# Index scores of a sparse attention layer: pairs of heads, and the keys' low parts on 64 rows

## The chip, the cores and the metric

The kernel runs on one core of a Trainium2 chip. The metric is the device time of one execution in microseconds. The kernel before was timed in three runs: 1888.56, 1888.76 and 1889.16 us, median 1888.76. One further execution was profiled; every row of the trace comes from it.

## What is computed

Two layers of a decoder for 512 tokens of width 2048, in float32. The first layer is a sparse attention whose "indexer" scores every key for every query and keeps the best 128; the second is a stick-breaking attention. Only the indexer matters here:

```python
iq = partial_rope(iq.reshape(b, s, IDX_HEADS, IDX_DIM), positions, IDX_ROT)   # 16 heads of 64
ik = partial_rope(ik.reshape(b, s, 1, IDX_DIM), positions, IDX_ROT)[:, :, 0, :]
...
dots = jnp.einsum('bqhd,bsd->bqhs', iqb, ik).astype(jnp.float32)
iscore = jnp.einsum('bqhs,bqh->bqs', jax.nn.relu(dots), iwb.astype(jnp.float32)) * idx_scale
iscore = jnp.where(causal[None], iscore, -jnp.inf)
_, idx = lax.top_k(iscore, n_sel)
```

Sixteen index heads of dimension 64 share one set of 512 index keys. For each query the products with the keys go through a ReLU, are weighted per head, and summed over the heads. Since 128 keys are kept, the first 128 queries keep all that they may see, and scores are needed only for the queries from 128 on.

## The kernel before, in words

All activations are held transposed: the 128 partitions carry features, the free axis carries the tokens. Matmuls run on operands rounded to a shorter float32 format (fp32r). To keep float32 accuracy each operand is split into a high part, the rounded value, and a low part, the rest (`split`, L129): ScalarE makes the high part, VectorE subtracts. A product then takes three matmuls, high × high, high × low and low × high (`mm3`, L133, lines L134 to L136), which accumulate in one PSUM bank. There are eight banks of 128 × 512.

TensorE's instructions stand in the order in which the program writes them. The other engines' instructions are put in order by a planner, except those written as "paced". Two devices mix independent work into TensorE's stream: `interleave` (L57) runs a main generator and lets a second one, the fill, advance by a given total over the main one's steps; `pumped` (L313) hands out one queued piece of work on the other engines at each step. Weights come over the SP queue into three raw buffers, are split into `wh` and `wl` (three buffers each), and are prepared two pieces ahead.

The index stage goes as follows.

- The index queries come out of the projection as `iq`, two heads of 64 rows in a 128-row bank. `index_piece` (L573) turns them and makes, for each head, a stack `sa` or `sb` of 128 rows: for an even head rows 0 to 63 hold the high part and rows 64 to 127 the low part; for an odd head it is the other way round.
- The index keys `ik` (64 rows) are made into two operands of 128 rows, `B1` and `B2` (L648 to L651). `B1` holds the keys' high part in rows 0 to 63 and their low part in rows 64 to 127; `B2` holds them the other way round.
- `index_scores` (L665) runs over three blocks of 128 queries (i = 1, 2, 3), which see w = 256, 384 and 512 keys, and over the 16 heads. A head takes one of three banks in turn (`spare`, L531), two matmuls of the stack with `B1` and with `B2` (L671, L672), which together give all four products of the parts, then a ReLU by ScalarE into `rl` (three buffers) and an accumulation by VectorE into `am[i]`.
- The fill is the projection of the values, `gemm_x` (L292), on banks 4 to 7: 64 steps of three 512-wide matmuls each, tile `v` in the trace. 22 steps run ahead of the scores, 40 are spread over them, and the rest follows.
- Behind the stage come the splits of the values (`vh`, `vl`) and the projection of the queries (tile `q`), whose first group uses banks 0 to 3. Bank 3 was last used by the index queries.

In the trace the score banks are called `isc`, the operands `B1` and `B2` together `B`.

Of the kernel before, what the change touches and what calls it, by code (L numbers as in the profile page):

```python
# [10 lines left out]
F32 = mybir.dt.float32  # L11
F32R = mybir.dt.float32r
I32 = mybir.dt.int32
AF = mybir.ActivationFunctionType
ALU = mybir.AluOpType
# [3 lines left out]
T = 512  # L19
# [27 lines left out]
def run(gen):  # L47
    for _ in gen:
        pass


def steps(gen, n):
    for _ in range(n):
        next(gen, None)


def interleave(main, n_main, fill, n_fill, lead=0):  # L57

    steps(fill, lead)
    done = 0  # L60
    for i, _ in enumerate(main, 1):
        steps(fill, n_fill * i // n_main - done)
        done = n_fill * i // n_main
    run(fill)
# [13 lines left out]
def trunk_kernel(  # L78
# [17 lines left out]
    pe = nc.tensor  # L96
# [21 lines left out]
    act, dve, pool = (Paced(e) for e in (nc.scalar, nc.vector, nc.gpsimd))  # L118
# [7 lines left out]
    def bank(i, name="ps"):  # L126
        return psum.tile([128, 512], F32, name=name, tag=f"bank{i}")
# [5 lines left out]
    def mm3(out, a, b, start, stop):  # L133
        pe.matmul(out, a[0], b[0], start=start, stop=False)  # L134
        pe.matmul(out, a[0], b[1], start=False, stop=False)  # L135
        pe.matmul(out, a[1], b[0], start=False, stop=stop)  # L136
# [155 lines left out]
    def gemm_x(items, get, banks):  # L292

        for kb in range(NK):
            w = next(items)
            xh, xl = get(kb)
            for t, out in enumerate(banks):
                s = slice(t * 128, (t + 1) * 128)
                mm3(out, (xh[:, s], xl[:, s]), w, kb == 0, kb == NK - 1)
                yield  # L300
# [9 lines left out]
    def one():  # L310
        paced(bg.popleft())

    def pumped(gen, every=1):  # L313

        for i, _ in enumerate(gen):
            if bg and i % every == 0:
                one()
            yield

    def drain():  # L320
        while bg:
            one()
# [35 lines left out]
    def strassen_stream(widths, wp):  # L358
        return Ahead(strassen_items(widths, wp), 2)
# [73 lines left out]
    def first_chunk(gemm, TF, T1, C3, stream):  # L433

        for k in range(8):
            if k < 7:
                if k > 0:
                    paced(build_plain, k + 1)
            else:
                items = stream().prime()  # L440
            steps(gemm, 4)
            if k < 4:
                for piece in stream_sums(k + 4, TF[k % 2], T1[k + 4], C3):
                    paced(piece)
                    steps(gemm, 2)
            else:
                steps(gemm, 4)
            if k:
                paced(turn_first, k - 1, T1[k - 1])
        run(gemm)  # L450
        turn_first(7, T1[7])
        return items
# [78 lines left out]
    def spare(name, first=4):  # L531
        spin[0] = (spin[0] + 1) % 3
        return bank(first + spin[0], name)

    def mm_banks(name):
        return [bank(j, name) for j in range(4)]
# [4 lines left out]
    am = [pa.tile([128, 128 * (i + 1)], F32, name=f"am{i}") for i in range(4)]  # L541
# [5 lines left out]
    def all_items():  # L547
        yield from first_items()
        yield from plain_items([(80, NK), *[(512, NK)] * 10])

    items = Ahead(all_items(), 2)

    pi_ = ExitStack()
    ip = pi_.enter_context(ss(name="pi", bufs=1, side="right"))
    Ci = ip.tile([128, T], F32, name="Ci")
    Si = ip.tile([128, T], F32, name="Si")
    B1 = ip.tile([128, T], F32R, name="B1")
    B2 = ip.tile([128, T], F32R, name="B2")
    iws = ip.tile([128, 3, 16], F32, name="iws")
    stacks = {}  # L560
# [48 lines left out]
    def late_banks(where):  # L609
        return [bank(b, "iq")[:, :LATE] for b in where]  # L610
# [14 lines left out]
    banks = late_banks((4, 5, 6, 7))  # L625
# [11 lines left out]
    ps = bank(4, "ik")  # L637
    run(pumped(gemm_w(items, plain, [ps], 80)))
    drain()
    ik = ip.tile([128, T], F32, name="ik")  # L640
# [4 lines left out]
    dve.tensor_tensor(iksw[0:32], iksw[0:32], Si[0:32], ALU.mult)  # L645
    dve.tensor_tensor(ik[0:32], ik[0:32], Ci[0:32], ALU.mult)
    dve.tensor_tensor(ik[0:32], ik[0:32], iksw[0:32], ALU.add)
    act.activation(B1[0:64], ik[0:64], AF.Copy)  # L648
    act.activation(B2[64:128], ik[0:64], AF.Copy)
    dve.tensor_tensor(B1[64:128], ik[0:64], B1[0:64].bitcast(F32), ALU.subtract)  # L650
    dve.tensor_tensor(B2[0:64], ik[0:64], B1[0:64].bitcast(F32), ALU.subtract)  # L651

    banks = late_banks(range(4))
    gemm = gemm_w(items, late_plain, banks)
# [10 lines left out]
    def index_scores():  # L665
        for i in range(1, 4):
            w = 128 * (i + 1)
            for h in range(16):
                ps = spare("isc", 0)
                st = stacks[h][:, (i - 1) * 128 : i * 128]  # L670
                pe.matmul(ps[:, :w], st, B1[:, :w], start=True, stop=False)  # L671
                pe.matmul(ps[:, :w], st, B2[:, :w], start=False, stop=True)  # L672
                rl = ip.tile([128, T], F32, name="rl", tag="rl", bufs=3)
                act.activation(rl[:, :w], ps[:, :w], AF.Relu)
                wcol = iws[:, i - 1, h : h + 1]
                if h == 0:
                    dve.tensor_scalar(am[i], rl[:, :w], wcol, None, ALU.mult)
                else:
                    dve.scalar_tensor_tensor(am[i], rl[:, :w], wcol, am[i], ALU.mult, ALU.add)
                yield  # L680
            diag = am[i][:, i * 128 : w]
            pool.affine_select(out=diag, in_=diag, pattern=[[-1, 128]], compare_op=ALU.is_ge, fill=FILL, base=0, channel_multiplier=1)
        pool.memset(am[0], 0.0)
        pool.affine_select(out=am[0], in_=am[0], pattern=[[-1, 128]], compare_op=ALU.is_ge, fill=MASK, base=0, channel_multiplier=1)

    banks = [bank(b, "v") for b in (4, 5, 6, 7)]
    interleave(index_scores(), 48, pumped(gemm_x(items, plain, banks)), 40, lead=22)
    drain()
    pi_.close()
    pkv_ = ExitStack()  # L690
# [48 lines left out]
    for g in range(4):  # L739
        banks = [bank(b + 4 * (g % 2), "q") for b in range(4)]  # L740
# [61 lines left out]
    for g in range(4):  # L802
        banks = mm_banks("g")
# [267 lines left out]
    with ps_:  # L1071
# [3 lines left out]
        banks = [bank(b, "k") for b in range(4)]  # L1075
        gemm = gemm_w(kitems, plain, banks, order=PAIRS)
        items = first_chunk(gemm, TF, T1, C3, lambda: strassen_stream([512] * 5, sp))
# [45 lines left out]
    def gate_items():  # L1123
        for k, n in ((0, 6), (4, 2)):
            yield from plain_items([(512, n)])
            raw = next_raw()
            bg.extend(lambda raw=raw, k=k: restore(raw, k) for k in range(k, k + 4))
        yield from plain_items([(512, 8), *[(512, NK)] * 3])

    items = Ahead(gate_items(), 2)  # L1130
# [14 lines left out]
    banks = mm_banks("g")  # L1145
# [79 lines left out]
    for g in range(4):  # L1225
        tc.keep_in_program_order(act.preload_act_table_set("natural_log_exp_and_others"))
        if g:
            banks = mm_banks("g")
# [63 lines left out]
```

## Time and profile before

| | us |
|---|---|
| median of three runs | 1888.76 |
| the profiled execution's own time | 1889.62 |
| its span in the trace | 1887.9 |
| first score matmul | 144.57 |
| first matmul behind the last score matmul | 188.45 |

A row of a timeline gives the start and the duration in us, the engine, the line, the operation, out<-in by the program's names, the shapes and a count; in square brackets stands the idle time ahead of it and what ended it. PE is TensorE's matmuls and PEld its weight loads, which run beside them; DVE is VectorE, ACT ScalarE, POOL GpSimd. Instructions that a helper issues all carry the helper's line: L111 for everything on ScalarE and VectorE.

### The profile page before, as it was taken

To read this page: it belongs to the slowest core of one execution; us is meant where nothing else is said; L and a number is where in the kernel's file an instruction comes from. 1 tells how busy PE (TensorE), PEld (TensorE's weight loads), DVE (VectorE), ACT (ScalarE), POOL (GpSimd) and SP (SyncE) were. 2 spreads that over 40 slices of the span, in tenths; PEclk is the share of its full clock that TensorE was granted. 3 is DMA by queue.
4 is the path that set the end of the run, shared out by engine and by line. 5 is a ranking of instruction groups with operands and counts; after the bars stand their busy time and mean duration, and the time that the engine had idled before them with its cause. 6 is when DMAs were issued, how large, how long until landed. Compare 5 with 4: busy or idle time off the path is not lost.

```text
span 1887.9 us, 25064 instructions
## 1 busy us (share of the span) xinstructions
PE 1874.2 (99%) x9229; PEld 1584.7 (84%) x9229; DVE 1220.4 (65%) x2385; ACT 928.5 (49%) x1692; POOL 28.4 (2%) x49
## 2 busy tenths in 40 slices
PE   9999999999999999999999999999999999999998
PEld 7898888888888888888888999987888888888887
DVE  5668879966556454675368788876655545567534
ACT  4446323355554432474245444468877743347422
POOL 0000000000000000000000000000100000000000
PEclk9999999999999999999999999999999999999999
DMA  5432333312222532333343333331122153242333
GB/s 185 137 114 65 101 90 100 101 56 68 67 68 60 165 110 78 124 100 106 117 134 113 106 97 111 101 112 57 56 68 68 57 189 98 75 129 89 123 101 112
DMA packets 110587, 189.22 MB, mean 100 GB/s; under 512 B 8240, under 2 KB 28208, under 8 KB 110464
## 3 DMA queue, kind: packets, MB, share of 16 engines
q1 hardware_dynamic: 110320, 187.33, 32.3%
q8 instruction: 72, 1.18, 0.3%
q14 instruction: 51, 0.42, 0.1%
q0 software_dynamic: 144, 0.30, 0.1%
HBM read 179.21 MB, written 8.39 MB: 99 GB/s over the span
## 4 chain that ended last, share of the span: by engine, by line
PE 96%; DVE 2%; ACT 1%; DMA 1%; issue 1%; SPq 0%; DVEq 0%; ACTq 0%
PE g L134 12%; PE g L135 12%; PE g L136 12%; PE o L135 7%; PE o L136 7%; PE o L134 7%; PE m L134 3%; PE m L135 3%; PE m L136 3%; PE q L135 3%; PE q L136 3%; PE q L134 3%; PE z L1199 2%; PE k L136 2%; PE k L135 2%; PE k L134 2%
## 5 line engine op out<-in xcount | busy, mean ns | idle before, releaser
L111 ACT ACTIVATE wh<-raw 128x512 fp32r<-128x512 f32 (+3 forms) x684 | 396.4, 581 | 674.9 <-PE g L135 239.4
L111 DVE TENSOR_TENSOR wl<-raw,wh 128x512 fp32r<-128x512 f32 (+3 forms) x684 | 430.0, 630 | 430.9 <-ACT wh L111 411.6
L134 PE MATMUL g<-xh,wh 128*128 128x512 f32 x1024 | 404.3, 395 | 0.2
L135 PE MATMUL g<-xl,wh 128*128 128x512 f32 x1024 | 400.6, 391 | 0.6 <-DVE xl L111 0.6
L136 PE MATMUL g<-xh,wl 128*128 128x512 f32 x1024 | 399.9, 391 | 0.0
L134 PEld LDWEIGHTS g<-xh,wh 128*128 128x128 f32 x1024 | 192.6, 188 | 41.0 <-ACT sg L111 1.4
L136 PEld LDWEIGHTS g<-xh,wl 128*128 128x128 f32 x1024 | 192.2, 188 | 41.2
L135 PEld LDWEIGHTS g<-xl,wh 128*128 128x128 f32 x1024 | 192.5, 188 | 38.7 <-DVE xl L111 1.4
L136 PE MATMUL o<-xh,wl 128*128 128x512 f32 x512 | 199.3, 389 | 0.0
L135 PE MATMUL o<-xl,wh 128*128 128x512 f32 x512 | 199.2, 389 | 0.0
L134 PE MATMUL o<-xh,wh 128*128 128x512 f32 x512 | 199.2, 389 | 0.0
L136 PEld LDWEIGHTS o<-xh,wl 128*128 128x128 f32 x512 | 96.1, 188 | 20.3 <-DVE wl L111 0.4
L135 PEld LDWEIGHTS o<-xl,wh 128*128 128x128 f32 x512 | 96.1, 188 | 20.0
L134 PEld LDWEIGHTS o<-xh,wh 128*128 128x128 f32 x512 | 96.1, 188 | 19.9
L134 PE MATMUL q<-xh,wh 128*128 128x512 f32 x256 | 99.6, 389 | 0.0
L135 PE MATMUL q<-xl,wh 128*128 128x512 f32 x256 | 99.6, 389 | 0.0
L136 PE MATMUL q<-xh,wl 128*128 128x512 f32 x256 | 99.6, 389 | 0.0
L111 ACT ACTIVATE sh<-st 128x512 fp32r<-128x512 f32 x80 | 49.0, 628 | 79.7 <-PE m L135 42.5
L111 DVE TENSOR_TENSOR sl<-st,sh 128x512 fp32r<-128x512 f32 x80 | 54.5, 691 | 37.2 <-ACT sh L111 37.2
L111 DVE TENSOR_TENSOR xl<-f,xh 128x512 fp32r<-128x512 f32 x80 | 54.3, 687 | 11.4 <-ACT f L111 11.0
L111 ACT ACTIVATE wk<-z 128x512 f32<-128x512 f32 x80 | 47.3, 591 | 25.2 <-PE z L136 17.2
L134 PEld LDWEIGHTS q<-xh,wh 128*128 128x128 f32 x256 | 48.1, 188 | 10.1
(290 smaller groups left out, 3366.8 us busy)
## 6 DMA issues: line engine op xcount, KB each, us to landing
raw<-w_in_a SPq DMA_DIRECT2D x95, 512.0 KB, 3.7
raw<-w_in_b SPq DMA_DIRECT2D x64, 512.0 KB, 3.8
raw<-w_ple_gate SPq DMA_DIRECT2D x52, 512.0 KB, 3.8
raw<-w_o_a SPq DMA_DIRECT2D x24, 512.0 KB, 3.8
raw<-w_o_b SPq DMA_DIRECT2D x24, 512.0 KB, 3.7
raw<-w_kv_b SPq DMA_DIRECT2D x16, 512.0 KB, 3.8
raw<-w_ple_gate SPq DMA_DIRECT2D x24, 256.0 KB, 2.9
f<-xT SPq DMA_DIRECT2D x4, 1024.0 KB, 6.2
```

The source lines that it names most:

```text
L111: ins = method(*args, **kw)
L134: pe.matmul(out, a[0], b[0], start=start, stop=False)
L135: pe.matmul(out, a[0], b[1], start=False, stop=False)
L136: pe.matmul(out, a[1], b[0], start=False, stop=stop)
L1199: pe.matmul(z, m, p, start=False, stop=n == len(terms), skip_group_check=True)
```

## The change

`B1` now holds the keys' high part in both halves of the rows, `B2` their low part in both halves. A head's first matmul, on all 128 rows, gives (query high + query low) × key high. Its second uses only the 64 rows of the stack that hold the query's high part, rows 0 to 63 for an even head and 64 to 127 for an odd one, and gives query high × key low. The product of the two low parts is left out.

Heads go in pairs: two full matmuls into two banks, then the two on 64 rows, then the two ReLUs and accumulations. The banks are 0 to 3 by the head's number. The fill's 40 steps are spread over 24 pairs in place of 48 heads.

```diff
-    act.activation(B1[0:64], ik[0:64], AF.Copy)
-    act.activation(B2[64:128], ik[0:64], AF.Copy)
-    dve.tensor_tensor(B1[64:128], ik[0:64], B1[0:64].bitcast(F32), ALU.subtract)
-    dve.tensor_tensor(B2[0:64], ik[0:64], B1[0:64].bitcast(F32), ALU.subtract)
+    for rows in (slice(0, 64), slice(64, 128)):
+        act.activation(B1[rows], ik[0:64], AF.Copy)
+        dve.tensor_tensor(B2[rows], ik[0:64], B1[0:64].bitcast(F32), ALU.subtract)
...
-            for h in range(16):
-                ps = spare("isc", 0)
-                st = stacks[h][:, (i - 1) * 128 : i * 128]
-                pe.matmul(ps[:, :w], st, B1[:, :w], start=True, stop=False)
-                pe.matmul(ps[:, :w], st, B2[:, :w], start=False, stop=True)
-                rl = ip.tile([128, T], F32, name="rl", tag="rl", bufs=3)
...
+            for pair in range(0, 16, 2):
+                heads = []
+                for h in (pair, pair + 1):
+                    ps = bank(h % 4, "isc")
+                    st = stacks[h][:, (i - 1) * 128 : i * 128]
+                    pe.matmul(ps[:, :w], st, B1[:, :w], start=True, stop=False)
+                    heads.append((h, ps, st))
+                for h, ps, st in heads:
+
+                    rows = slice(64 * (h % 2), 64 * (h % 2) + 64)
+                    pe.matmul(ps[:, :w], st[rows], B2[rows, :w], start=False, stop=True)
+                for h, ps, _ in heads:
+                    rl = ip.tile([128, T], F32, name="rl", tag="rl", bufs=3)
+                    act.activation(rl[:, :w], ps[:, :w], AF.Relu)
...
-    interleave(index_scores(), 48, pumped(gemm_x(items, plain, banks)), 40, lead=22)
+    interleave(index_scores(), 24, pumped(gemm_x(items, plain, banks)), 40, lead=22)
```

More of the change, by code (lines that the diff above doesn't have):

```diff
@@ L667, in index_scores @@
             w = 128 * (i + 1)
-            for h in range(16):
-                ps = spare("isc", 0)
-                st = stacks[h][:, (i - 1) * 128 : i * 128]
-                pe.matmul(ps[:, :w], st, B1[:, :w], start=True, stop=False)
-                pe.matmul(ps[:, :w], st, B2[:, :w], start=False, stop=True)
-                rl = ip.tile([128, T], F32, name="rl", tag="rl", bufs=3)
[L674 to L679, printed above, removed]
+            for pair in range(0, 16, 2):
[11 more added lines that the diff above has]
+                    act.activation(rl[:, :w], ps[:, :w], AF.Relu)
+                    wcol = iws[:, i - 1, h : h + 1]
+                    if h == 0:
+                        dve.tensor_scalar(am[i], rl[:, :w], wcol, None, ALU.mult)
+                    else:
+                        dve.scalar_tensor_tensor(am[i], rl[:, :w], wcol, am[i], ALU.mult, ALU.add)
                 yield
```

## The prediction

> **What bounds the kernel now.** I read the head of the page first, then the chain that ended last, then the busy times cut at the borders of the stage that the change touches.
>
> ```profile
> span 1887.9 us, 25064 instructions
> PE 1874.2 (99%) x9229; PEld 1584.7 (84%) x9229; DVE 1220.4 (65%) x2385; ACT 928.5 (49%) x1692; POOL 28.4 (2%) x49
> PEclk9999999999999999999999999999999999999999
> PE 96%; DVE 2%; ACT 1%; DMA 1%; issue 1%; SPq 0%; DVEq 0%; ACTq 0%
> ```
>
> TensorE is busy for 99% of the span at the full granted clock, and 96% of the last chain is its own work. The stage of the index scores is no exception. The next rows cut it by the widths of the scores (256, 384 and 512 keys); the columns after the first comma are the busy time and count of PE, PEld, DVE, ACT and POOL, then the clock.
>
> ```profile
> 144.57:158.68 14.11, 14.11 (x80) 12.33 (x79) 11.65 (x24) 9.00 (x23) 0.29 (x1) 1.00 0.26 76
> 158.68:173.34 14.66, 14.66 (x71) 12.77 (x71) 11.56 (x20) 9.57 (x20) 0.31 (x1) 1.00 0.25 73
> 173.34:188.45 15.11, 15.11 (x67) 12.21 (x65) 12.34 (x19) 9.71 (x17) 0.37 (x1) 1.00 0.12 35
> ```
>
> PE fills all 43.88 us; VectorE has 35.55 us of work in them (81%), ScalarE 28.28 us (64%). So a matmul slot saved or added here moves everything behind it, until VectorE has no room left. The instructions that write or read the score banks confirm it:
>
> ```profile
> L111 ACT ACTIVATE rl<-isc x48: 365/491/600, 145.0 to 188.6; 128x256 f32<-128x256 f32 x16, 128x384 f32<-128x384 f32 x16, 128x512 f32<-128x512 f32 x16
> L671 PEld LDWEIGHTS isc<-B,sa x24: 187/188/188, 144.3 to 186.6; 128*128 128x128 f32 x24
> L672 PE MATMUL isc<-B,sa x24: 278/332/398, 144.7 to 187.1; 128*128 128x256 f32 x8, 128*128 128x384 f32 x8, 128*128 128x512 f32 x8
> L111 DVE SCALAR_TENSOR_TENSOR am<-rl,iws,am x45: 477/618/753, 146.0 to 189.3; 128x256 f32<-128x256 f32 x15, 128x384 f32<-128x384 f32 x15, 128x512 f32<-128x512 f32 x15
>   PE isc L672: 14.0, 27
> ```
>
> The last row says who waits for whom: ScalarE stood idle 14.0 us, 27 times, until a score matmul was done. TensorE waits for neither of the other two here.
>
> **The price of a matmul slot.** Durations overlap (a 512-wide matmul is drawn with 0.39 us but the next one starts 0.23 us later), so slots are taken from start to start.
>
> ```profile
> 144.57 0.28 PE L671 MATMUL isc<-B,sa 128*128 128x256 f32 x1
> ...
> 144.92 0.28 PE L672 MATMUL isc<-B,sb 128*128 128x256 f32 x1
> 145.04 0.39 PE L134 MATMUL v<-wh,xh 128*128 128x512 f32 x1
> ...
> 159.37 0.34 PE L671 MATMUL isc<-B,sa 128*128 128x384 f32 x1
> ...
> 159.89 0.34 PE L672 MATMUL isc<-B,sb 128*128 128x384 f32 x1
> 160.07 0.40 PE L134 MATMUL v<-wh,xh 128*128 128x512 f32 x1
> ...
> 187.98 0.40 PE L671 MATMUL isc<-B,sb 128*128 128x512 f32 x1
> 188.22 0.39 PE L672 MATMUL isc<-B,sb 128*128 128x512 f32 x1
> 188.45 0.40 PE L134 MATMUL v<-wh,xh 128*128 128x512 f32 x1
> ```
>
> Four 256-wide slots take 145.04 − 144.57 = 0.47 us, 0.118 each; four 384-wide ones 0.70 us, 0.175 each; two 512-wide ones 0.47 us, 0.235 each.
>
> **What the change removes.** A pair of heads now issues four full matmuls. Afterwards it issues two full ones and two on 64 rows each. The halves use different rows of the array and write different banks. If they run side by side, a pair takes three slots, and with 8 pairs at each width the gain is 8 × (0.118 + 0.175 + 0.235) = 4.22 us. No row here shows two matmuls side by side, so the bounds are that gain and zero, if the second half takes a slot of its own. I take side by side, since the two share neither rows nor a bank. The number of matmuls, weight loads, activations and accumulations doesn't change.
>
> **What it adds: two changes of the array's shape in every pair.** Ahead of the halves the array works as one block of 128 rows; then as two of 64, each with its own sums going out; then as one again for the V matmuls, of which one or two groups of three follow each pair (40 groups on 24 pairs). That makes 48 changes in 24 pairs. A sum on its way through all 128 rows can't cross a border that ends it at row 64, so I expect the array to run empty at each change. No matmul in this trace has fewer than 128 rows, so the price is bounded.
>
> From below: nothing. From above: the overlap of neighbouring matmuls is lost and the load of the weights too. The overlap is duration less slot: 0.28 − 0.118, 0.34 − 0.175, 0.39 − 0.235 in the rows above, 0.16 each time (with the caveat that ends of matmuls are modelled). For a load:
>
> ```profile
> 144.57 0.19 PEld L672 LDWEIGHTS isc<-B,sa 128*128 128x128 f32 x1
> 144.69 0.19 PEld L671 LDWEIGHTS isc<-B,sb 128*128 128x128 f32 x1
> L134 PEld LDWEIGHTS ik<-xh,wh x16: 147/148/148, 84.7 to 95.0; 128*80 128x80 f32 x16
> 84.66 0.39 PE L136 MATMUL k<-xh,wl 128*128 128x512 f32 x1
> 84.89 0.40 PE L134 MATMUL ik<-xh,wh 128*80 128x512 f32 x1
> ```
>
> Each load starts with the matmul ahead of it (144.57, 144.69) and is hidden by it. 128 columns take 188 ns and 80 take 148, so a column costs 40 / 48 = 0.83 ns and 128 of them 0.107 us. The change from 128 to 80 columns keeps the slot, 84.89 − 84.66 = 0.23 us, which speaks for the lower bound. The upper bound of one change is then 0.16 + 0.107 = 0.27 us.
>
> The nearest row of a change in what the array does is at the transposes of the attention stage, which sit in such a stream:
>
> ```profile
> 390.64 0.40 PE L136 MATMUL g<-xh,wl 128*128 128x512 f32 x1
> 390.88 0.60 PE L786 MATMUL pt<-ident,p 128*128 128x128 f32 x4
> 391.23 0.47 PE L134 MATMUL g<-xh,wh 128*128 128x512 f32 x1
> 391.54 0.39 PE L135 MATMUL g<-xl,wh 128*128 128x512 f32 x1
> 391.20 0.19 PEld L134 LDWEIGHTS g<-xh,wh 128*128 128x128 f32 x1
> ```
>
> Going in costs nothing (390.88 − 390.64 = 0.24); the first matmul behind them holds its slot for 0.31 instead of 0.23 us, and its load started only 0.03 us ahead of it. So a load that isn't hidden costs 0.08 us, and a transpose, which uses the whole array, does not empty it. I therefore don't take the transposes' near-zero for the change of shape, but use their 0.08 for a load that comes late. I take 0.16 for each of the two changes, and 0.08 once in a pair: on the way in two loads (2 × 0.107 us) stand behind one matmul of 0.118 to 0.235 us, on the way out one load stands behind the two halves. That is 0.40 us for a pair, 24 × 0.40 = 9.6 us in all; the bounds are 0 and 24 × 2 × 0.27 = 13.0 us.
>
> Beside this stands the Trainium skill, TensorEngine Tiling (Array Packing), section Tiling Modes: going from one tiling mode to another, not merely to another tile, makes TensorE drain first. No run here shows it. By that rule the overlap of 0.16 us is lost twice a pair and the sum is the forecast's or more; without it the sum would be the gain alone. Of the loads the Trainium skill, TensorE: Matmul & The Clock Gate, section Part 2: What happens when you issue a matmul, says that their time goes by columns and not by rows. The rows for 128 and 80 columns agree as to columns, and none shows fewer rows; by it the four loads of a 256-wide pair, 4 × 0.107 us, allow only 0.04 us of gain there, which would make the whole gain 3.6 instead of 4.2 us.
>
> **What it moves.** The operands' two copies and two subtractions are reordered and write other rows, four instructions as before:
>
> ```profile
> 100.89 1.29 ACT L111 ACTIVATE B<-ik 64x512 fp32r<-64x512 f32 x2
> 101.56 1.38 DVE L111 TENSOR_TENSOR B<-ik,B 64x512 fp32r<-64x512 f32 x2
> L111 ACT ACTIVATE irw<-iq x8: 483/490/492, 78.0 to 130.2; 128x384 f32<-128x384 f32 x8
> 190.53 0.39 PE L134 MATMUL q<-xh,wh 128*128 128x512 f32 x1
> ```
>
> They end at 102.9 us and are used at 144.57. The 41 us of matmuls between hide any order of them; uncovered they'd cost about 2.7 us. The scores now use banks 0 to 3 in place of 0 to 2. Bank 3 was emptied by about 130.7 us and is wanted again by the fourth group of the q matmuls, 3 × 0.69 us after 190.53; the last head's activation starts at 188.6 and takes 0.60, so some 3 us of V and q matmuls cover it, and a wait there would be at most the lateness of that activation. The removed calls of the three-bank counter number 48, a multiple of three, so later banks stay the same. No DMA is added or passed. Activations and accumulations now come two at a time behind both halves, which lets one stand behind the other for 0.6 to 0.8 us; four banks and three activation buffers take that up. All this I put at zero.
>
> **The sum.** 9.6 − 4.2 = +5.4 us on the stage and on the end. The profiled execution took 1889.62 us with its span of 1887.9; it becomes 1895.0. The runs have a median of 1888.76, 0.86 below it, so the forecast is 1894.2 us.
>
> **The rivals.** (1) *The change of shape is free, and the halves run side by side*: −4.2 us, 1884.6. For it speaks that neither 80 columns nor the way into a transpose costs anything; against it, that neither changes where sums end. It decides when a change costs under 4.2 / 48 = 0.09 us, and is a gain that can be told only under 0.01 us. (2) *Only a late load*, 0.08 us a pair, as behind the transposes: 1.9 − 4.2 = −2.3, 1886.5. (3) *The halves take turns and the array runs empty too*: +9.6, 1898.4. Both matmuls end in the same engine's stream, which shows no two at once so far. (4) *The change doesn't do what it says*: the halves take turns and nothing is emptied, ±0, 1888.8. (5) *VectorE becomes the bound* in the 512-wide part after a free change of shape:
>
> ```profile
> 184.14 2.46 DVE L111 SCALAR_TENSOR_TENSOR am<-rl,iws,am 128x512 f32<-128x512 f32 x3 [0.23 <-ACT rl L111]
> L111 DVE TENSOR_TENSOR wl<-raw,wh 128x512 fp32r<-128x512 f32 x11 | 7.6, 690 | 1.3 <-ACT wh L111 1.3
> ```
>
> Back to back an accumulation takes 2.46 / 3 = 0.82 us, 16 of them 13.1 us, and three low parts of weights 2.1 us: 15.2 us, while TensorE alone would need 15.11 − 8 × 0.235 = 13.2. If buffers took up none of that, the 1.9 us of this part would be lost: −2.3, 1886.5. Against it: the banks and buffers hold about four heads.
>
> **How the numbers follow.** Chances: forecast 0.45, with its own range from 48 × 0.16 − 4.2 = +3.5 to 13.0 − 4.2 = +8.8, 1892.3 to 1897.6; rival 1 0.15, rival 2 0.16, rival 3 0.11, rival 4 0.07, rival 5 0.06. The bound for telling a change from none is 0.2%, 3.8 us. Faster: rival 1 but for 0.01, 0.14. Slower: the forecast but for 0.01, and rival 3, 0.55. Same: the rest, 0.31. The range reaches from rival 1, 1884.4, to the cheaper part of rival 3, 1900; beyond lie its dearest cases.
>
> **What would show it.** The stage from the first score matmul to the last, 43.88 us, becomes 49.3; TensorE stays granted at full clock. Starts of two halves within a few ns show them side by side, a distance of 0.118 to 0.235 us shows turns. The slot of the second full matmul should grow by 0.16 to 0.24 us, that of the second half by 0.16; slots unchanged there make rival 1 or 2 true. A wait of a score matmul for ScalarE's activation would show rival 5. The forecast is wrong if the stage is under 44 us, or if the time outside the stage moves by more than 1 us.

## The result, and the profile after

The changed kernel takes 1894.39 us (median of nine runs, 1893.42 to 1896.05), the kernel before 1888.71 in its nine: a ratio of 1.0029 with a 95% interval of 1.0021 to 1.0038 (the intervals behind the ratios below are of the same kind). It is slower by 5.7 us, where 5.4 were forecast.

The head of the profile after shows as full a TensorE as before, and the same number of instructions on it:

```profile
span 1892.3 us, 25063 instructions
PE 1879.3 (99%) x9229; PEld 1580.9 (84%) x9229; DVE 1221.4 (65%) x2385; ACT 927.6 (49%) x1692; POOL 28.8 (2%) x49
PE 96%; DVE 2%; ACT 1%; issue 0%; DMA 0%; SPq 0%; DVEq 0%; ACTq 0%
```

Nothing here says where the time went: an array that waits between two matmuls is still drawn as busy. The starts of the matmuls say it. This is TensorE's timeline of a pair at 256 keys and of one at 512 in the changed kernel; L672 are the full matmuls, L677 those on 64 rows.

```profile
144.54 0.28 PE L672 MATMUL isc<-B,sa 128*128 128x256 f32 x1
144.66 0.28 PE L672 MATMUL isc<-B,sb 128*128 128x256 f32 x1
144.87 0.38 PE L677 MATMUL isc<-B,sa 64*128 64x256 f32 x1
144.87 0.38 PE L677 MATMUL isc<-B,sb 64*128 64x256 f32 x1
145.18 0.50 PE L134 MATMUL v<-wh,xh 128*128 128x512 f32 x1
145.52 0.39 PE L135 MATMUL v<-wl,xh 128*128 128x512 f32 x1
...
176.03 0.39 PE L672 MATMUL isc<-B,sa 128*128 128x512 f32 x1
176.26 0.40 PE L672 MATMUL isc<-B,sb 128*128 128x512 f32 x1
176.59 0.49 PE L677 MATMUL isc<-B,sa 64*128 64x512 f32 x1
176.59 0.49 PE L677 MATMUL isc<-B,sb 64*128 64x512 f32 x1
177.01 0.50 PE L134 MATMUL v<-wh,xh 128*128 128x512 f32 x1
177.35 0.39 PE L135 MATMUL v<-wl,xh 128*128 128x512 f32 x1
```

The halves start together, so the slot is saved as forecast. But three slots have grown, two of the pair and the one behind it. At 256 keys the second full matmul holds 0.21 us instead of 0.118 (+0.09), the halves 0.31 instead of 0.118 (+0.19), and the first V matmul 0.34 instead of 0.23 (+0.11). At 512 keys they hold 0.33 instead of 0.235 (+0.10), 0.42 instead of 0.235 (+0.19), and again 0.34 (+0.11). That is 0.39 to 0.40 us a visit whatever the width (a visit is one stay in the 64-row shape, from the change into it to the change out of it), against one saved slot of 0.118 to 0.235 us.

The weight loads of the pair at 512 keys show a second thing beside the wait:

```profile
176.03 0.19 PEld L672 LDWEIGHTS isc<-B,sb 128*128 128x128 f32 x1
176.59 0.18 PEld L677 LDWEIGHTS isc<-B,sa 64*128 64x128 f32 x1 [0.36 <-issue]
176.59 0.18 PEld L677 LDWEIGHTS isc<-B,sb 64*128 64x128 f32 x1
177.01 0.19 PEld L134 LDWEIGHTS v<-wh,xh 128*128 128x128 f32 x1 [0.24 <-issue]
177.12 0.19 PEld L135 LDWEIGHTS v<-wl,xh 128*128 128x128 f32 x1
```

Within a shape a load starts with the matmul ahead of it, as the second full one at 176.03 does. At a change it doesn't: the halves' loads start at 176.59 with their own matmuls, and the V load at 177.01 with its own. So the load stands open, hidden by no matmul, at both changes. The two halves' loads start together, as their matmuls do.

The whole stage, from the first score matmul to the first q matmul, is the cleanest measure, since the V matmuls in it are the same (126 in both traces). It went from 190.53 − 144.57 = 45.96 us to 195.88 − 144.54 = 51.34, +5.38 us:

```profile
195.88 0.39 PE L134 MATMUL q<-xh,wh 128*128 128x512 f32 x1
```

The rest of the span got shorter by 0.98 us (1841.94 to 1840.96), nearly all of it behind the stage (1697.37 to 1696.42). That part has the same code in all ten traces and takes 1696.4 to 1697.7 us in them, so this is a difference between executions. The profiled execution of the kernel before was itself 0.9 us over its median, so the spans differ by 4.4 us and the medians by 5.7.

### The profile page after: what moved, and what is told of

Read it like the earlier page. It is cut to its first block, busy times and chain, and to the rows that moved or that the text cites. A ratio compares the mean times of both kernels' runs of the same rounds, so it can differ in the third digit from the quotient of the medians.

```text
span 1892.3 us, 25063 instructions
## 1 busy us (share of the span) xinstructions
PE 1879.3 (99%) x9229; PEld 1580.9 (84%) x9229; DVE 1221.4 (65%) x2385; ACT 927.6 (49%) x1692; POOL 28.8 (2%) x49
## 4 chain that ended last, share of the span: by engine, by line
PE 96%; DVE 2%; ACT 1%; issue 0%; DMA 0%; SPq 0%; DVEq 0%; ACTq 0%
PE g L134 12%; PE g L135 12%; PE g L136 12%; PE o L135 7%; PE o L136 7%; PE o L134 7%; PE m L134 3%; PE m L135 3%; PE m L136 3%; PE q L136 3%; PE q L134 3%; PE q L135 3%; PE z L1205 2%; PE k L136 2%; PE k L135 2%; PE k L134 2%
## 5 line engine op out<-in xcount | busy, mean ns | idle before, releaser
L135 PEld LDWEIGHTS q<-xl,wh 128*128 128x128 f32 x256 | 48.1, 188 | 10.0
```

## The experiments

**The 64 rows undone, all else kept (e1).**

```diff
-                    rows = slice(64 * (h % 2), 64 * (h % 2) + 64)
-                    pe.matmul(ps[:, :w], st[rows], B2[rows, :w], start=False, stop=True)
+                    pe.matmul(ps[:, :w], st, B2[:, :w], start=False, stop=True)
```

> The changed kernel with the second matmul of each head back on all 128 rows (it then adds the product of the two low parts too); pairs, banks, the operands' new layout and the fill stay. Theory (the cost is the array's change of shape, twice a pair): no change of shape is left and no slot is saved, so the time of the kernel before, 1888.7 us within 1 us, and slots of 0.118, 0.175 and 0.235 us throughout. Rival (the order in pairs, the four banks or the coarser fill cost the time): it stays near the changed kernel's 1894.4 us.

Measured: 1889.01 us against 1889.13, a ratio of 0.9999 (0.9990 to 1.0008). The stage takes 45.91 us, as before (45.96). Pairs, banks, operands and the coarser fill cost nothing that can be told; all of the loss belongs to the matmuls on 64 rows.

**Both halves on the same rows (e2).**

```diff
-                    rows = slice(64 * (h % 2), 64 * (h % 2) + 64)
+                    rows = slice(0, 64)
```

> The changed kernel with both halves of a pair on rows 0 to 63, so that they can't run side by side (the odd heads then multiply their query's low part with the keys' low part, another product). The number of changes of shape stays at 48. Theory (the halves do run side by side in the changed kernel): each pair pays one slot more, 8 x (0.118 + 0.175 + 0.235) = 4.2 us, so 1898.6 us; the second half starts a slot behind the first. Rival (equal starts in the trace are only how it is recorded, and the halves take turns anyway): unchanged, 1894.4 us.

Measured: 1898.16 us, a ratio of 1.0047 (1.0033 to 1.0061). TensorE's timeline of this kernel at 512 keys:

```profile
178.34 0.40 PE L672 MATMUL isc<-B,sb 128*128 128x512 f32 x1
178.67 0.49 PE L677 MATMUL isc<-B,sa 64*128 64x512 f32 x1
179.00 0.39 PE L677 MATMUL isc<-B,sb 64*128 64x512 f32 x1
179.33 0.50 PE L134 MATMUL v<-wh,xh 128*128 128x512 f32 x1
```

Now the second half starts 0.33 us behind the first. The two take 0.66 us where the changed kernel's two took 0.42: one slot more. So the equal starts above are real. Over the 24 pairs the halves hold 13.2 us here and 8.9 in the changed kernel, so running side by side is worth 4.3 us in the slots (4.2 expected); the medians differ by 3.8 us.

**Four heads to a visit (e3).**

```diff
-            for pair in range(0, 16, 2):
+            for pair in range(0, 16, 4):
...
-                for h in (pair, pair + 1):
+                for h in range(pair, pair + 4):
...
-    interleave(index_scores(), 24, pumped(gemm_x(items, plain, banks)), 40, lead=22)
+    interleave(index_scores(), 12, pumped(gemm_x(items, plain, banks)), 40, lead=22)
```

> The changed kernel with four heads at a time: four full matmuls, then four halves, 12 groups and so 24 changes of shape in place of 48; the 40 steps of the fill are spread over the 12 groups. Theory (0.40 us for each visit to 64 rows, whatever is done there): 12 x 0.40 = 4.8 us of cost against the same 4.2 us of gain, so 0.6 us over the kernel before, 1889.3 us. Inside a visit the second two halves start one slot behind the first two, their loads hidden. Rival (each half matmul or its load costs, not the change of shape): as the changed kernel, 1894.4 us. Rival (four heads at once make the score banks wait for ScalarE's activations): waits of a score matmul for rl appear, and the time lies above 1889.3 us by their sum.

Measured: 1889.23 us, a ratio of 1.0001 (0.9992 to 1.0009). With as many halves as the changed kernel and half the visits the loss is gone, so the price is one of the visit and not of the matmul. No wait for an activation appears. Its timeline also takes the halves' 0.19 us apart:

```profile
177.17 0.40 PE L672 MATMUL isc<-B,sb 128*128 128x512 f32 x1
177.50 0.49 PE L677 MATMUL isc<-B,sa 64*128 64x512 f32 x1
177.50 0.49 PE L677 MATMUL isc<-B,sb 64*128 64x512 f32 x1
177.83 0.39 PE L677 MATMUL isc<-B,sa 64*128 64x512 f32 x1
177.84 0.39 PE L677 MATMUL isc<-B,sb 64*128 64x512 f32 x1
178.16 0.50 PE L134 MATMUL v<-wh,xh 128*128 128x512 f32 x1
```

The first two halves hold 177.83 − 177.50 = 0.33 us, 0.10 over a plain slot: their open load. The last two hold 178.16 − 177.84 = 0.32 us, 0.09 over it: the wait for the next change, while their own loads (177.60 and 177.61) lie behind the first two halves. A change is therefore about 0.09 us of waiting and 0.10 to 0.11 us of load.

**Twice as many changes (e4).** Each half stands behind its own full matmul, in one loop over the heads:

```diff
                     heads.append((h, ps, st))
-                for h, ps, st in heads:
-
                     rows = slice(64 * (h % 2), 64 * (h % 2) + 64)
```

> The changed kernel with each head's half directly behind its full matmul (full, half, full, half), so 96 changes of shape and no two halves next to each other. Theory (0.20 us for each change of shape): nothing is saved and 96 x 0.20 = 19.2 us are paid, so 1907.9 us. Rival (the cost belongs to the visit's first load or to the pair, not to every change): 48 x 0.40 would fall short of that, with 1898.6 us if only the lost slot counts.

Measured: 1908.38 us, a ratio of 1.0100 (1.0086 to 1.0113). 96 changes cost 1908.38 − 1889.13 = 19.25 us, 0.20 us each. A price by the pair falls, as 24 × 0.40 us would be 9.6. A price by the visit isn't told apart by the time, though the expectation takes it to be: each half is a visit of its own here, and 48 × 0.40 us is the same 19.2. That the way in and the way out both cost is read from the slots, here at 384 keys:

```profile
176.41 0.34 PE L672 MATMUL isc<-B,sa 128*128 128x384 f32 x1
176.68 0.44 PE L675 MATMUL isc<-B,sa 64*128 64x384 f32 x1
177.04 0.44 PE L672 MATMUL isc<-B,sb 128*128 128x384 f32 x1
177.42 0.44 PE L675 MATMUL isc<-B,sb 64*128 64x384 f32 x1
177.79 0.50 PE L134 MATMUL v<-wh,xh 128*128 128x512 f32 x1
178.12 0.39 PE L135 MATMUL v<-wl,xh 128*128 128x512 f32 x1
```

The first full matmul has a change only behind it and holds 0.27 us instead of 0.175 (+0.09, the wait). The next three have one on either side and hold 0.36 to 0.38 us (about +0.19 to +0.20, open load and wait). The V matmul has one only ahead of it and holds 0.33 us instead of 0.23 (+0.10, the open load). So every change costs.

**A shorter load (e5).** The first matmul closes its accumulation and the half adds to it, on 80 columns:

```diff
-                    pe.matmul(ps[:, :w], st, B1[:, :w], start=True, stop=False)
+                    pe.matmul(ps[:, :w], st, B1[:, :w], start=True, stop=True)
...
-                    pe.matmul(ps[:, :w], st[rows], B2[rows, :w], start=False, stop=True)
+                    pe.matmul(ps[:80, :w], st[rows, :80], B2[rows, :w], start=False, stop=True, skip_group_check=True)
```

> The changed kernel with the matmuls on 64 rows cut to 80 of their 128 columns (the low-part product is then left out for the last 48 queries of each block). Theory (a change of shape costs two things, a wait of 0.093 us until the array is empty, seen in the slot of the second full matmul, and the new weights' load that can then no longer be hidden, 0.107 us for 128 columns, at both changes): the wait stays, 0.209 us from the second full 256-wide matmul to the halves, and the halves' slot falls by 48 x 0.83 ns = 0.04 us, from 0.314 to 0.274 us; in all 24 x 0.04 = 1.0 us less than the changed kernel, 1893.4 us. Rival (a fixed restart of the array, with no load in it): slot and time unchanged.

Measured: 1893.20 us, a ratio of 1.0022 (1.0013 to 1.0031). In its timeline at 256 keys:

```profile
145.25 0.28 PE L672 MATMUL isc<-B,sb 128*128 128x256 f32 x1
145.46 0.34 PE L677 MATMUL isc<-B,sa 64*80 64x256 f32 x1
145.46 0.34 PE L677 MATMUL isc<-B,sb 64*80 64x256 f32 x1
145.73 0.50 PE L134 MATMUL v<-wh,xh 128*128 128x512 f32 x1
```

The wait ahead of the halves is unchanged (145.46 − 145.25 = 0.21 us), and the halves' slot is 0.27 instead of 0.31 us; over the 24 pairs the halves hold 0.9 us less than in the changed kernel (1.0 expected). So the part that goes by columns is the load; the part that doesn't is the wait.

**Fewer columns, all rows (e6).** The first matmul closes its accumulation here too.

```diff
-                    pe.matmul(ps[:, :w], st, B1[:, :w], start=True, stop=False)
+                    pe.matmul(ps[:, :w], st, B1[:, :w], start=True, stop=True)
...
-                    rows = slice(64 * (h % 2), 64 * (h % 2) + 64)
-                    pe.matmul(ps[:, :w], st[rows], B2[rows, :w], start=False, stop=True)
+                    pe.matmul(ps[:64, :w], st[:, :64], B2[:, :w], start=False, stop=True, skip_group_check=True)
```

> The changed kernel with the second matmuls on all 128 rows but only 64 columns, both of a pair on the same ones (the low-part product is then left out for the last 64 queries of each block). No two can run side by side, so no slot is saved. Theory (any smaller shape of the array costs the change, be it in rows or in columns): 24 visits of 2 x 0.093 + 0.053 + 0.107 = 0.35 us, 8.3 us over the kernel before, 1897.0 us. Rival (only the split of the rows costs, since sums then end elsewhere): near the kernel before, 1888.7 us, as for the 80 columns in its trace.

Measured: 1888.47 us, a ratio of 0.9998 (0.9989 to 1.0007). Here my theory was too wide and the rival held. The timeline at 512 keys has plain slots of 0.23 us on either side of the change:

```profile
176.94 0.39 PE L672 MATMUL isc<-B,sb 128*128 128x512 f32 x1
177.17 0.39 PE L676 MATMUL isc<-B,sa 128*64 128x512 f32 x1
177.40 0.40 PE L676 MATMUL isc<-B,sb 128*64 128x512 f32 x1
177.63 0.39 PE L134 MATMUL v<-wh,xh 128*128 128x512 f32 x1
```

Matmuls on 64 columns and all rows mix freely with full ones. What costs is the shape of 64 rows; e2 pays for it too, though only rows 0 to 63 work there.

**Halves only where a slot is dear (e7, e8).** Groups of four with halves at 512 keys, pairs of full matmuls at 256 and 384:

```diff
-            for pair in range(0, 16, 2):
+            n = 4 if i == 3 else 2
+            for pair in range(0, 16, n):
...
-                    rows = slice(64 * (h % 2), 64 * (h % 2) + 64)
+                    rows = slice(64 * (h % 2), 64 * (h % 2) + 64) if i == 3 else slice(0, 128)
...
-    interleave(index_scores(), 24, pumped(gemm_x(items, plain, banks)), 40, lead=22)
+    interleave(index_scores(), 20, pumped(gemm_x(items, plain, banks)), 40, lead=22)
```

> Halves only where a slot is worth most: groups of four heads with halves for the 512 keys, pairs of full matmuls for 256 and 384 keys. Theory: four visits of 0.40 us against 4 x 2 x 0.235 = 1.88 us saved, 0.3 us less than the kernel before, 1888.4 us, which is less than a measurement can tell. From first to last score matmul's end with the same V matmuls between, the last block gives 0.28 us less. Rival (four heads of 512 keys make the score banks wait): above the kernel before by those waits.

Measured: 1889.94 us, a ratio of 1.0005 (0.9996 to 1.0014). The second rival is what the timeline shows: with only two groups of V matmuls behind each four heads, the score banks are not free in time.

```profile
186.14 0.40 PE L673 MATMUL isc<-B,sa 128*128 128x512 f32 x1
187.04 0.50 PE L673 MATMUL isc<-B,sb 128*128 128x512 f32 x1 [0.51 <-ACT rl L111]
```

The bracket names ScalarE's activation; the slot is 0.90 us instead of 0.23. One more slot, at 182.62, holds 0.46 us. So 0.90 us are lost against about 0.28 gained, and the stage takes 46.61 us instead of 45.96. A last kernel gives each group of four twice the fill, with the total of the main steps back at 24:

```diff
-                yield
+                for _ in range(n // 2):
+                    yield
```

> As e7, with the fill given by heads and not by groups, so that a group of four at 512 keys gets 3 or 4 groups of V matmuls behind it in place of 2. Theory (e7's waits of the score banks for ScalarE, 0.67 and 0.23 us, came from too little other work between its groups): the waits are gone, and from the first score matmul to the first q matmul 0.3 us less than the 45.96 us of the kernel before, about 45.7; the time 1888.4 us, not to be told from the kernel before. Rival (four heads at once are too many for ScalarE and VectorE in any case): waits of a score matmul for rl stay, and the stage is 46.0 us or more.

Measured: 1888.63 us against 1888.69, a ratio of 0.9999 (0.9990 to 1.0008). No score matmul waits any more, and the stage ends earlier, at

```profile
144.69 0.28 PE L673 MATMUL isc<-B,sa 128*128 128x256 f32 x1
...
190.22 0.39 PE L134 MATMUL q<-xh,wh 128*128 128x512 f32 x1
```

45.53 us against 45.96 before. Not all of this 0.43 us is the change's. In e6, which saves no slot, the stage is shorter too:

```profile
144.80 0.28 PE L672 MATMUL isc<-B,sa 128*128 128x256 f32 x1
...
190.43 0.39 PE L134 MATMUL q<-xh,wh 128*128 128x512 f32 x1
```

That is 45.63 us; its V matmuls, the same ones as before, hold 0.230 us on average, and those of the kernel before 0.232. By its own slots, e8's score matmuls at 512 keys hold 6.76 us instead of 7.43, and the four V matmuls behind its visits 0.10 us more each. So about 0.26 us is left of the idea (0.28 expected), and neither the stage nor the kernel's time can tell it from none.

## Why the prediction was right

**The bound.** TensorE's own chain carried the stage, and the loss went through to the end: +5.38 us in the stage, +5.7 in the medians. Neither VectorE nor ScalarE holds TensorE in the changed kernel's stage: its trace shows no wait there.

**The gain.** The halves run side by side, as taken; their starts lie together in the rows of after, and e2 prices it at 4.3 us in the slots and 3.8 in the medians, against a forecast of 4.22. Rivals 3 and 4, that they take turns, fall. So does the smaller gain of 3.6 us that four loads one after another would have left: the loads of the two halves start together (at 144.87 in the pair at 256 keys), and their slot has grown by one open load, not by two.

**The price of a visit.** 0.40 us was forecast, 0.39 to 0.40 is seen. That a change of shape costs TensorE a wait and an open load was right. That the total fits so closely is luck, since both parts were off. The step "I take 0.16 for each of the two changes, and 0.08 once in a pair" has the wait too dear and the load too cheap: the wait is 0.09 us (second full matmul after, and e5), and the load costs 0.10 to 0.11 at both changes, not once. I had let the load on the way out hide behind the halves; the rows show that no load crosses a change of shape in either direction. The 0.08 us itself came from a load that started 0.03 us ahead of its matmul; one without a head start costs more. The waits came out 2 × 0.07 us below the forecast and the loads 0.13 us above it, and the two errors cancel. The wait was taken from the modelled ends of the matmuls, which lie 0.07 us behind the start of the next shape's load (144.66 + 0.28 = 144.94 against 144.87).

The Trainium skill, TensorEngine Tiling (Array Packing), section Tiling Modes, says that a change of mode drains TensorE and gives no price. The wait of 0.09 us at each change, the same for all widths, agrees with it; that the array empties in that time is argued, as no row shows the inside of the array. Its list of modes has 128 rows by 64 columns too; matmuls of that size cost nothing in e6, but whether they ran in that mode the trace doesn't say.

**The rivals.** A free change of shape (1) and a late load alone (2) fall by the grown slots, and e4's slots put the price at 0.20 us a change. VectorE as the bound (5) was not reached in the changed kernel, since its visits leave more time than before; a kin of it, ScalarE holding the score banks, came in e7, where the groups were large and the fill short.

**What was moved.** The order of the operands, the banks and the fill were put at zero; e1 confirms it within 0.1%.

**The markers.** The slot of the second full matmul was to grow by 0.16 to 0.24 us and grew by 0.09 to 0.10; the halves' was to grow by 0.16 and grew by 0.19. These misses are the two wrong parts above. A stage of 49.3 us from the first score matmul to the V matmul behind the last was announced; by that border it is 193.01 − 144.54 = 48.47, since the coarser fill leaves one V group of 0.70 us more behind the border and the last open load, 0.11, falls there too.

```profile
193.01 0.50 PE L134 MATMUL v<-wh,xh 128*128 128x512 f32 x1
```

## What to carry to other kernels

Two matmuls on half the rows do run at once, but going into that shape and out of it costs 0.20 us each way in a dense stream, 0.09 of waiting and 0.11 of weights that can't be loaded ahead. Count visits, not matmuls: a visit has to save more than 0.40 us, here two 512-wide slots, so gather at least four such halves between two changes, and see that the banks they fill are emptied in time. Even four gained next to nothing: e3 about broke even, and e8's 0.26 us can't be told from none. A profile that reads 99% busy before and after hides all of this; compare starts of neighbouring instructions.

## What was not expected of the hardware

Matmuls on fewer columns can be mixed with full ones at no cost (e6: slots of 0.23 us on both sides), and matmuls on half the rows can't. A load for half the rows, which no row of before showed, takes nearly as long as one for all of them, 183 against 188 ns in the changed kernel:

```profile
L672 PEld LDWEIGHTS isc<-B,sa x24: 187/188/188, 144.3 to 191.8; 128*128 128x128 f32 x24
L677 PEld LDWEIGHTS isc<-B,sa x24: 182/183/183, 144.9 to 192.6; 64*128 64x128 f32 x24
```
